# One block of a hybrid encoder on one core: three attention and gate steps, one load's page and some weight offsets in other places

## The chip, the cores and the metric

The kernel runs on one core of a Trainium2 chip. The metric is the device time of one execution in microseconds (us); of several runs the median counts. The kernel before has three runs: 2178.95, 2183.16 and 2185.89 us, median 2183.16.

## The reference, cut to what matters

One layer of a hybrid block on 512 frames of 2048 channels, all in float32:

```python
h = rms_norm(x, norm_mix_w)
q_a, k_a, v_a, q_g, k_g, v_g, r_g, gate_lr = split_cols(h @ w_in, IN_SPLITS)   # 6160 columns
y_a = chunked_band_attention(q_a, k_a, v_a, att_rel_bias)    # 16 heads of 64
o_g = gated_linear_attention(q_g, k_g, v_g, log_a)           # 4 heads, chunk by chunk
y_g = rms_norm(o_g, gla_norm_w) * silu(r_g)
x = x + concat([y_a, y_g]) @ w_out
u = causal_depthwise_conv(rms_norm(x, norm_ffn_w) @ w_ffn_up, w_ffn_conv, b_ffn_conv)
u_gate, u_val = split(u, 2)                                  # 5632 columns each
x = x + (gelu(u_gate) * u_val) @ w_ffn_down
g = sigmoid(rms_norm(x, norm_ple_w) @ w_ple_gate)
x = x + g * (p @ w_ple_proj)
out = rms_norm(x, final_norm_w)
```

In the attention a query sees its own chunk of 64 frames and the eight before it, with a learned bias by relative distance, and a softmax over them.

## The kernel before, in words

**Units, products, steps.** Nearly all time goes into matrix products. A unit makes two blocks of 128 output columns for all 512 frames. It does so with seven products of half-sized operands instead of eight (Strassen's scheme): P1, P2, P6, P5, P7, P3, P4, of which some take a sum of two weight blocks (S1 to S4) and some a sum or difference of two input blocks (N1, N2, T3, T4). A product is one step of a list of 704 steps (`steps`). In it TensorE runs 24 matmuls of 128 by 256 columns: eight blocks of the contraction, three times over, first the weights' high part with the input's high part, then the high part with the input's low part, then the weights' low part with the input's high part. So the low weights are first read by the 17th matmul.

The stages follow each other: `front` (the projection w_in; gate units and attention pairs), `pp` (per-layer embedding), `wo`, `up`, `dn0` to `dn2`, `pg`. The steps that matter here: 0 to 41 the linear-attention units, 42 to 90 the attention pairs' projections, 84 to 111 the gate units 0 to 3, 112 to 115 `pp`, 116 on `wo`, 172 on `up`, 648 on `pg`.

**Weights.** A block of weights (`l`, 512 KB) comes from memory into a page. Sums (`s`) are made by a load with an accumulating second DMA on GpSimd's queue, or on VectorE. Two steps ahead of a step, ACT copies the raw block into a high part (`w<-l`, `w<-s`) and VectorE subtracts it to give the low part (`w<-l,w`, `w<-s,w`). Both go to one of three slots, used in turn (step number modulo 3); a slot starts at 1024 columns times its number plus an offset, 24 unless `places` gives another for that step (line 546). `place` fills that table (line 983).

**Attention.** `attend(unit)` (line 810) gives a list of work items for one pair of heads: `high`, `low` and `low_copy` split the queries and keys, then three turns h, one for each of three groups of query tiles: `scores` (TensorE, `psc`), `soft` (VectorE and ACT), `normal` (VectorE divides by the sums), `turn` (TensorE transposes the result, `ptr`) and `evict` (ACT copies the transposes to `PT`), and at the end `values` (TensorE, `py`) and `result`. Turn 1 uses the buffer `scb`, turns 0 and 2 `sc`. Pair 0's items are counted from step 38, pair 7's from step 84.

**Gates.** A gate unit g (0 to 3) has its result multiplied by the linear attention's output, which lies in memory (`ond`). `load_on` (line 925) loads it into a page `on` of 512 KB; `after_gates` then has VectorE multiply (`u<-u,on`) and `store_pair` makes four sums (`tp`) and stores seven blocks of 128 KB (`mix_R..`, `mix_N..`, `mix_T..`) for the next stage. `page(ring, ...)` takes the next page of a ring of named pages: ring "c" has three pages at that place, ring "x" two.

**The order.** Each item has a step and a key: key 0 is before the split of the weights two steps ahead, 1 between its halves, 2 to 8 behind the step's matmuls, 9 after ACT or VectorE has added the product to its unit. TensorE, ACT and VectorE run in the order that this list gives, and each waits at its first unready instruction. Transfers are issued by SP, and accumulating ones by GpSimd; their order is made by a scheduler from its own estimates, so an edit can move a transfer past others. SP waits at the first one whose page, source or completion count isn't ready, and everything behind it waits too. Eight completion counters are used in turn, so an issue also waits for the landing of the eighth one before it.

Of the kernel before, what the change touches and what calls it, by code (L numbers as in the profile page):

```python
# [42 lines left out]
def encoder_block(ctx: ExitStack, tc: tile.TileContext, A, out):  # L43
# [5 lines left out]
    pg = ctx.enter_context(tc.tile_pool(name="pages", bufs=1))  # L49
# [53 lines left out]
    def page(ring, name, dt=F32, shape=(P, 1024)):  # L103
        tags = rings[ring]
        i = counts.get(ring, 0)
        counts[ring] = i + 1
        tag = tags[i % len(tags)]
        return page_pool(tag).tile(list(shape), dt, tag=tag, name=name)
# [3 lines left out]
    def page_pool(tag):  # L112
        return late[0] if tag in LATE else pg
# [221 lines left out]
    def xtile(op, g, name, dt=F32R):  # L335
        if (op, g) not in H_TAGS:
            return xa[0].tile([P, 2, 1024], dt, tag=f"{op}{g}", name=name)
        c = 2048 * H_TAGS.index((op, g))
        return h_all[:, c:c + 2048].rearrange("p (h n) -> p h n", h=2)
# [473 lines left out]
    def attend(unit):  # L813
        b, M = unit.u, {}
        o = unit.o

        def tile_(name, cols, dt=F32, tag=None, bufs=1):
            return att[0].tile([P, cols], dt, tag=tag or name, name=name, bufs=bufs)
# [8 lines left out]
        def high(s):  # L827
            for n in ("Q", "Kh", "Kl"):
                M[n, s] = tile_(f"{n}{s}", T + 64, F32R)[:, 16:16 + T] if n == "Q" else tile_(f"{n}{s}", T, F32R)
            a = slice(s * 64, s * 64 + 64)  # L830
            act.activation(M["Q", s][a], o[a, 0, :], AF.Copy, scale=0.125)
            for r in (a, slice(64 - s * 64, 128 - s * 64)):
                act.activation(M["Kh", s][r], o[a, 1, :], AF.Copy)
# [71 lines left out]
        def result():  # L905
            if b % 2 == 0:
                ypair[:] = [page("c", "yp").rearrange("p (s t) -> p s t", s=2)]
            act.activation(ypair[0][:, b % 2, :], M["y"], AF.Copy)

        done = 13 if b < 3 else 14 if b < 7 else 10  # L910
        items = [(2 + (b == 1), 7, load_e if b else lambda: None), (2, 2, lambda: high(0)), (2, 9, lambda: high(1)), (3, 1, low), (4, 2, low_copy), (9 - b // 7, 0, load_v),
                 (done, 4, values), (done + 1, 1, result)]
        if b % 2:
            items.append((done + 2, 1, lambda: store_pair(mixd, b // 2, ypair[0][:, 0, :], ypair[0][:, 1, :])))
        z = b == 0
        for h in range(3):
            t = (7 + z, 9 if b < 7 else 8, 11 if b < 7 else 9)[h]
            items += [(t, k, lambda f=f, h=h: f(h)) for t, k, f in (
                (5 + h + z * (h == 2), 6, scores), (6 + h + z * (h == 2), 1, soft), ((7, 8, 10 if b < 7 else 9)[h], 1, normal),
                (t, 5, turn), (t + 1, 1, evict))]  # L920
        return items

# [1 line left out]

    def load_on(unit):
        g = unit.u - 8
        unit.on = page("x" if g == 0 else "c", "on").rearrange("p (s t) -> p s t", s=2)
        nc.sync.dma_start(unit.on, ond[g])

    def after_gates(unit):  # L930
        g = unit.u - 8

        def times():
            vec.tensor_tensor(unit.o, unit.o, unit.on, ALU.mult)

        def pair():
            ops = store_pair(mixd if g < 2 else None, 4 + g, unit.o[:, 0, :], unit.o[:, 1, :])
            if g >= 2:
                tails[g - 2] = ops

        load = [] if g == 2 else [(0, 0, lambda: load_on(unit))]
        return load + [(0, 1, lambda: act.activation(unit.o, unit.o, AF.Silu)), (2 * (g in (1, 2)), 2, times), (2 * (g in (1, 2)), 3, pair)]
# [25 lines left out]
    wo = stages[2]  # L968
    units = [u for st in stages for u in st.units]
    steps = []  # L970
    base = {}
# [9 lines left out]
    places = {}  # L981

    def place(i):
        places[i + (1 - i) % 3] = 0

    for unit, at in ((front.units[13], 1), (front.units[14], -2)):
        place(base[unit] + at)
    plain = [i for i, (_, p) in enumerate(steps) if p == "PP"]
    for i in plain:
        if i % 3 < 2:  # L990
            places[i] = (72, 8)[i % 3]
    for st in stages[2:]:
        for at in (0 if st.name == "wo" else 3, *range(13 if st.name == "up" else 16, 7 * len(st.units) - 14, 21)):
            place(base[st.units[0]] + at)

    agenda = [[] for _ in range(len(steps) + 60)]
    now = [0]
    for a, b in zip(stages[2:], stages[3:]):
        i0 = base[a.units[-1]]
        for n, p in enumerate(PLAIN):  # L1000
            op = PRODUCTS[p][1]
            for g in range(2):
# [3 lines left out]
                at = 2 * n + (11 if g else 8)  # L1006
                k = 3
                if g and b.chained and op in ("R21", "T4"):
                    at, k = max(at, 15), 0 if op == "R21" else 3
                if b.chained and op == "N1":  # L1010
                    at = 17 + g
# [110 lines left out]
    for n in range(2):  # L1122
        u = stages[-1].units[n - 2]
        at = end + 4 + n
# [517 lines left out]
    agenda[base[front.units[4]] + 9].append((0, first_bias))  # L1642
    agenda[base[front.units[4]] + 12].append((0, open_attention))
    agenda[base[front.units[14]] + 5].append((0, lambda: load_on(front.units[14])))
    use_rings(FRONT_RINGS)
    for i, (unit, prod) in enumerate(steps[:-4]):
        st = unit.stage
# [21 lines left out]
        if i - len(steps) in EARLY:  # L1669
            p, op, g = EARLY[i - len(steps)]  # L1670
            t = xtile(op, g, "last")
# [247 lines left out]
```

## Time and profile before

| | before |
|---|---|
| median of three runs | 2183.16 us |
| the profiled execution | 2181.47 us, its span 2179.7 us |
| mean granted clock of TensorE | 0.998 |
| TensorE busy | 2167.8 us, 99% |
| VectorE busy | 1860.8 us, 85% |
| ACT busy | 1333.4 us, 61% |
| DMA | 566.64 MB, 55.4% of 16 engines by SP's and ACT's queue, 31.0% by GpSimd's |

The span is the time from the first to the last instruction of one execution; a share is of that span. The granted clock is 1.00 at 2.4 GHz, and a mean between 0.5 and 1.00 is a stretch with some of it at 1.2 GHz. In timelines, the number in front is the start in us, then comes the duration, the engine, the line, the operation and "out<-in" by the names in the program; in brackets behind it, how long the engine idled before and what ended that. "x24" is 24 instructions in a row. A step's matmuls overlap, so the ends that the rows give run over into the next step's start; the distance of two starts is the cadence.

### The profile page before, as it was taken

The page shows a single profiled execution, that of the slowest core. Times are in us where ns is not written, and L with a number is a line of the kernel's source. Part 1 is how long each engine was busy: PE and PEld are TensorE (multiplying, and loading weights), DVE is VectorE, ACT ScalarE, POOL GpSimd, SP SyncE. Part 2 cuts the span into 40 slices and gives each one's busy share as a digit, 9 for nine tenths or more (in the row PEclk, how much of TensorE's full clock was granted, in tenths as well). Part 3 has the DMA queues.
Part 4 walks back from the last instruction along what each step waited for, and adds up shares of the span by engine and source line. Part 5 has one row for each costly group of instructions (what it writes and reads, how often), then busy time and mean ns, then how long its engine had stood idle before and what let it go on. Part 6 is the DMA issues. An engine that isn't in the chain of part 4 may idle for free.

```text
span 2179.7 us, 45707 instructions
## 1 busy us (share of the span) xinstructions
PE 2167.8 (99%) x18262; PEld 2123.8 (97%) x18262; DVE 1860.8 (85%) x2549; ACT 1333.4 (61%) x1976; POOL 216.2 (10%) x263
## 2 busy tenths in 40 slices
PE   9999999999999999999999999999999999999998
PEld 7889999999999999999999999999999999999998
DVE  6977778888698889999888888888898687898998
ACT  6664567876665765555555555555564554666766
POOL 1111011111100001110111111011100101000010
PEclk9999999999999999999999999999999999999999
DMA  7988788889978978999999989989986976979996
GB/s 245 271 220 232 217 242 227 231 245 251 365 272 266 363 223 240 269 265 262 261 239 261 257 257 252 257 244 250 270 302 187 309 222 178 332 247 341 304 291 230
DMA packets 199973, 566.64 MB, mean 260 GB/s; under 512 B 22384, under 2 KB 61552, under 8 KB 199760
## 3 DMA queue, kind: packets, MB, share of 16 engines
q1 hardware_dynamic: 163232, 436.00, 55.4%
q0 software_dynamic: 34944, 125.32, 31.0%
q8 instruction: 143, 2.34, 0.4%
q10 hardware_dynamic: 1584, 2.40, 0.3%
q14 instruction: 70, 0.57, 0.1%
HBM read 490.23 MB, written 127.93 MB: 284 GB/s over the span
## 4 chain that ended last, share of the span: by engine, by line
PE 96%; DVE 2%; ACT 1%; DMA 1%; issue 1%; POOL 0%; ACTq 0%; DVEq 0%; POOLq 0%
PE accA L64 48%; PE accC L64 24%; PE accB L64 12%; PE v L64 4%; PE vaA L64 2%; PE pp L64 1%; PE vaC L64 1%; PE py L64 1%; PE psc L64 1%; PE ptr L64 1%; PE po L64 1%; PE vaD L64 0%; PE vaB L64 0%; DMA s<-in_w_blk 0%; DVE w L64 0%
## 5 line engine op out<-in xcount | busy, mean ns | idle before, releaser
L64 PE MATMUL accA<-h,w 128*128 128x256 f32 x5088 | 612.2, 277 | 0.2
L64 PEld LDWEIGHTS accA<-h,w 128*128 128x128 f32 x5088 | 594.6, 188 | 1.7 <-ACT u L64 0.3
L64 DVE TENSOR_TENSOR w<-s,w 128x1024 fp32r<-128x1024 f32 (+1 forms) x381 | 457.5, 1202 | 81.6 <-ACT w L64 81.1
L64 PE MATMUL accC<-h,w 128*128 128x256 f32 x4248 | 509.0, 276 | 0.0
L64 PEld LDWEIGHTS accC<-h,w 128*128 128x128 f32 x4248 | 494.2, 188 | 0.3
L64 DVE TENSOR_TENSOR w<-l,w 128x1024 fp32r<-128x1024 f32 (+1 forms) x320 | 383.1, 1197 | 63.3 <-ACT w L64 61.8
L64 ACT ACTIVATE w<-l 128x1024 fp32r<-128x1024 f32 (+1 forms) x320 | 332.3, 1039 | 165.6 <-PE accC L64 112.3
L64 ACT ACTIVATE w<-s 128x1024 fp32r<-128x1024 f32 (+1 forms) x381 | 395.0, 1037 | 23.5 <-PE accB L64 11.6
L64 ACT ACTIVATE u<-accA 128x256 f32<-128x256 f32 x302 | 114.5, 379 | 365.1 <-PE accA L64 362.5
L64 DVE TENSOR_TENSOR s<-s,l 128x1024 f32<-128x1024 f32 (+1 forms) x176 | 211.3, 1201 | 9.9 <-DMA s<-in_w_blk 7.7
L64 POOL DMA_DIRECT2D s<-in_w_up x84 | 73.3, 872 | 742.0 <-DMA s<-in_w_up 224.2
L64 DVE SCALAR_TENSOR_TENSOR cv<-u,cw,cv 128x511 f32<-128x511 f32 (+1 forms) x176 | 131.6, 748 | 3.1
L64 PE MATMUL accB<-up_R,w 128*128 128x256 f32 x1056 | 127.7, 277 | 0.0
L64 PE MATMUL accA<-up_R,w 128*128 128x256 f32 x1056 | 126.7, 276 | 0.0
L64 PE MATMUL accA<-up_N,w 128*128 128x256 f32 x1056 | 126.5, 276 | 0.0
L64 PEld LDWEIGHTS accB<-up_R,w 128*128 128x128 f32 x1056 | 124.0, 188 | 0.0
L64 PEld LDWEIGHTS accA<-up_R,w 128*128 128x128 f32 x1056 | 122.9, 188 | 0.0
L64 PEld LDWEIGHTS accA<-up_N,w 128*128 128x128 f32 x1056 | 122.8, 188 | 0.0
L64 ACT ACTIVATE u<-accC 128x256 f32<-128x256 f32 x98 | 37.5, 383 | 94.4 <-PE accC L64 94.1
L64 PE MATMUL v<-w,h 128*128 128x512 f32 x384 | 88.1, 390 | 0.1
L64 PEld LDWEIGHTS v<-w,h 128*128 128x128 f32 x384 | 71.8, 188 | 15.6 <-ACT g_t L64 0.5
L64 ACT ACTIVATE cv<-u,cw 128x512 f32<-128x512 f32 x88 | 67.1, 810 | 28.1 <-DVE u L64 26.6
(315 smaller groups left out, 2834.2 us busy)
## 6 DMA issues: line engine op xcount, KB each, us to landing
l<-in_w_up SPq DMA_DIRECT2D x132, 512.0 KB, 7.3
s<-in_w_up SPq DMA_DIRECT2D x84, 512.0 KB, 4.8
s<-in_w_up POOLq DMA_DIRECT2D x84, 512.0 KB, 7.0
l<-in_w_dn SPq DMA_DIRECT2D x56, 448.0 KB, 5.5
l<-in_w_blk SPq DMA_DIRECT2D x48, 512.0 KB, 6.0
s<-in_w_blk SPq DMA_DIRECT2D x32, 512.0 KB, 4.8
s<-in_w_blk POOLq DMA_DIRECT2D x32, 512.0 KB, 7.9
l<-in_w_out SPq DMA_DIRECT2D x28, 512.0 KB, 4.9
```

The costliest lines, as they stand in the source:

```text
L64: ins = f(*args, **kw)
```

## The change

Four things are edited.

- Pair 0 (b = 0): the second turn comes one step later, at step 48 instead of 47, and `high(1)` has another key. Pair 7 (b = 7): the second turn comes at step 93 instead of 92, the third at 94 instead of 93, the values at 95 instead of 94; the normalising stays.
- Gate unit 1's load takes a page of ring "x" instead of "c". The units 2 and 3 thereby get other pages of "c".
- A place is given by the step itself, with offset 64 in the third slot and 0 in the first, where it was always the second slot with 0.
- The places: 117 (offset 64) instead of 118 in `wo`, 186 (64) instead of 187 and every 21 steps from 211 instead of 208 in `up`, and a new 661 in `pg`. The others stay.

```diff
--- before.py
+++ after.py
@@ -907,16 +907,16 @@
                 ypair[:] = [page("c", "yp").rearrange("p (s t) -> p s t", s=2)]
             act.activation(ypair[0][:, b % 2, :], M["y"], AF.Copy)
 
-        done = 13 if b < 3 else 14 if b < 7 else 10
-        items = [(2 + (b == 1), 7, load_e if b else lambda: None), (2, 2, lambda: high(0)), (2, 9, lambda: high(1)), (3, 1, low), (4, 2, low_copy), (9 - b // 7, 0, load_v),
+        done = 13 if b < 3 else 14 if b < 7 else 11
+        items = [(2 + (b == 1), 7, load_e if b else lambda: None), (2, 2, lambda: high(0)), (2, 9 if b else 2, lambda: high(1)), (3, 1, low), (4, 2, low_copy), (9 - b // 7, 0, load_v),
                  (done, 4, values), (done + 1, 1, result)]
         if b % 2:
             items.append((done + 2, 1, lambda: store_pair(mixd, b // 2, ypair[0][:, 0, :], ypair[0][:, 1, :])))
         z = b == 0
         for h in range(3):
-            t = (7 + z, 9 if b < 7 else 8, 11 if b < 7 else 9)[h]
+            t = (7 + z, 9 + z, 10 + (b < 7))[h]
             items += [(t, k, lambda f=f, h=h: f(h)) for t, k, f in (
-                (5 + h + z * (h == 2), 6, scores), (6 + h + z * (h == 2), 1, soft), ((7, 8, 10 if b < 7 else 9)[h], 1, normal),
+                (5 + h + z * (h == 2), 6, scores), (6 + h + z * (h == 2), 1, soft), ((7, 8, 9 + (b < 7))[h], 1, normal),
                 (t, 5, turn), (t + 1, 1, evict))]
         return items
 
@@ -924,7 +924,7 @@
 
     def load_on(unit):
         g = unit.u - 8
-        unit.on = page("x" if g == 0 else "c", "on").rearrange("p (s t) -> p s t", s=2)
+        unit.on = page("x" if g < 2 else "c", "on").rearrange("p (s t) -> p s t", s=2)
         nc.sync.dma_start(unit.on, ond[g])
 
     def after_gates(unit):
@@ -981,17 +981,23 @@
     places = {}
 
     def place(i):
-        places[i + (1 - i) % 3] = 0
+        places[i] = (64, 0)[i % 3]
 
     for unit, at in ((front.units[13], 1), (front.units[14], -2)):
-        place(base[unit] + at)
+        place(base[unit] + at + (1 - base[unit] - at) % 3)
     plain = [i for i, (_, p) in enumerate(steps) if p == "PP"]
     for i in plain:
         if i % 3 < 2:
             places[i] = (72, 8)[i % 3]
     for st in stages[2:]:
-        for at in (0 if st.name == "wo" else 3, *range(13 if st.name == "up" else 16, 7 * len(st.units) - 14, 21)):
-            place(base[st.units[0]] + at)
+        b0 = base[st.units[0]]
+        for at in (1 if st.name == "wo" else 3, *range(16, 7 * len(st.units) - 14, 21)):
+            place(b0 + at + ((1 - b0 - at) % 3 if at > 1 else 0))
+        if st.name in ("up", "pg"):
+            after = max(i for i in places if i <= b0 + 18)
+            place(after - (4 if st.name == "up" else 3))
+            if st.name == "up":
+                del places[after]
 
     agenda = [[] for _ in range(len(steps) + 60)]
     now = [0]
```

TensorE's order around the first pair's second and third turn (`scb` the second, `sc` the third, `acc` the steps' matmuls; steps 47 to 49), before:

```order
L64 MATMUL accC<-in_R_1043,w 128x256 x2
L64 MATMUL ptr<-ident,scb 128x128 x6
L64 MATMUL accA<-h_100,w 128x256 x24
L64 MATMUL accA<-in_R_643,w 128x256 x4
L64 MATMUL accA<-in_R_760,w 128x256 x4
...
L64 MATMUL accA<-in_R_760,w 128x256 x4
L64 MATMUL ptr<-ident,sc 128x128 x6
L64 MATMUL psc<-Kh_3352,Q_3351 128x512
```

and now:

```order
L64 MATMUL accC<-in_R_1043,w 128x256 x2
L64 MATMUL accA<-h_100,w 128x256 x24
L64 MATMUL ptr<-ident,scb 128x128 x6
L64 MATMUL accA<-in_R_643,w 128x256 x4
L64 MATMUL accA<-in_R_760,w 128x256 x4
...
L64 MATMUL accA<-in_R_760,w 128x256 x4
L64 MATMUL ptr<-ident,sc 128x128 x6
L64 MATMUL psc<-Kh_3352,Q_3351 128x512
```

The six transposes of the second turn have moved behind the whole step 48; the third turn stays where it was, now with only step 49 between.

TensorE's order at the last pair (`py` the values), steps 92 to 95, before:

```order
L64 MATMUL accB<-in_R_1043,w 128x256 x2
L64 MATMUL ptr<-ident,scb 128x128 x6
L64 MATMUL accA<-h_100,w 128x256 x24
L64 MATMUL ptr<-ident,sc 128x128 x6
L64 MATMUL accC<-h_100,w 128x256 x24
L64 MATMUL py<-PT,va 64x128 x20
L64 MATMUL accA<-h_100,w 128x256 x24
L64 MATMUL accC<-in_R_671,w 128x256 x2
```

and now:

```order
L64 MATMUL accB<-in_R_1043,w 128x256 x2
L64 MATMUL accA<-h_100,w 128x256 x24
L64 MATMUL ptr<-ident,scb 128x128 x6
L64 MATMUL accC<-h_100,w 128x256 x24
L64 MATMUL ptr<-ident,sc 128x128 x6
L64 MATMUL accA<-h_100,w 128x256 x24
L64 MATMUL py<-PT,va 64x128 x20
L64 MATMUL accC<-in_R_671,w 128x256 x2
```

Both turns and the values stand one step later.

VectorE's order at the last pair's sums (`tp_6047` before, `tp_6090` now) and gate 0's multiply (`on_6097`, now `on_6085`), before:

```order
L64 TENSOR_TENSOR w_99<-l22_5642,w_99 128x1024
L64 TENSOR_TENSOR u_5842<-u_5842,accA_5776 128x256
L64 TENSOR_TENSOR tp_6047<-yp_5847 128x256 x2
L64 SCALAR_TENSOR_TENSOR tp_6047<-tp_6047,yp_5847 128x256 x2
L64 TENSOR_TENSOR w_99<-l11_5716,w_99 128x1024
L64 TENSOR_TENSOR u_5842<-u_5842,accC_5968 128x256
L64 TENSOR_TENSOR s2_6099<-s1_5912,l11_5716 128x1024
L64 TENSOR_TENSOR w_99<-l12_5875,w_99 128x1024
L64 TENSOR_TENSOR u_5464<-u_5464,on_6097 128x1024
```

and now:

```order
L64 TENSOR_TENSOR w_99<-l22_5642,w_99 128x1024
L64 TENSOR_TENSOR u_5842<-u_5842,accA_5776 128x256
L64 TENSOR_TENSOR w_99<-l11_5716,w_99 128x1024
L64 TENSOR_TENSOR u_5842<-u_5842,accC_5958 128x256
L64 TENSOR_TENSOR s2_6087<-s1_5904,l11_5716 128x1024
L64 TENSOR_TENSOR tp_6090<-yp_5847 128x256 x2
L64 SCALAR_TENSOR_TENSOR tp_6090<-tp_6090,yp_5847 128x256 x2
L64 TENSOR_TENSOR w_99<-l12_5875,w_99 128x1024
L64 TENSOR_TENSOR u_5464<-u_5464,on_6085 128x1024
```

The four `tp` instructions stand behind the S2 sum now.

SP's order at the gates' loads (`on_6142` is gate 1's, `on_6309` and `on_6602` those of 2 and 3; `l12_6090`, now `l12_6078`, is a later unit's block; `u_5464`, `tp_6129` are gate 0's results), before:

```order
L64 DMA l11_6088<-in_w_blk 128x1024
L310 DMA mix_N10_118<-tp_6047 128x256
L310 DMA mix_T30_120<-tp_6047 128x256
L310 DMA mix_N20_122<-tp_6047 128x256
L310 DMA mix_T40_124<-tp_6047 128x256
L928 DMA on_6142<-ond_202 128x1024
L64 DMA s3_6176<-in_w_blk 128x1024
L64 DMA l12_6090<-in_w_blk 128x1024
L310 DMA mix_R111_113<-u_5464 128x256
L310 DMA mix_R211_115<-u_5464 128x256
L310 DMA mix_R221_117<-u_5464 128x256
```

and now:

```order
L64 DMA l11_6076<-in_w_blk 128x1024
L928 DMA on_6085<-ond_202 128x1024
...
L928 DMA on_6309<-ond_202 128x1024
L928 DMA on_6602<-ond_202 128x1024
L310 DMA mix_N10_118<-tp_6090 128x256
...
L310 DMA mix_T40_124<-tp_6090 128x256
L64 DMA s3_6176<-in_w_blk 128x1024
L310 DMA mix_R111_113<-u_5464 128x256
...
L310 DMA mix_T41_125<-tp_6129 128x256
L928 DMA on_6142<-ond_202 128x1024
L64 DMA l22_6206<-in_w_blk 128x1024
L64 DMA l11_6210<-in_w_ple_proj 128x1024
```

Gate 1's load stood ahead of S3 and gate 0's stores and now stands behind them; the loads of the gates 2 and 3, which came after row `l11_6282` some twenty places later, are ahead of it; L11 of the next unit (`l11_6076`) is ahead of gate 0's load.

## Rows read from the trace of the kernel before

**Rows 1.** The page: engines' busy time; then the chain's shares by engine.

```profile
PE 2167.8 (99%) x18262; PEld 2123.8 (97%) x18262; DVE 1860.8 (85%) x2549; ACT 1333.4 (61%) x1976; POOL 216.2 (10%) x263
...
PE 96%; DVE 2%; ACT 1%; DMA 1%; issue 1%; POOL 0%; ACTq 0%; DVEq 0%; POOLq 0%
```

**Rows 2.** Three windows, one step each: us, PE busy, PEclk, DMA share, GB/s.

```profile
788.13:790.96 2.83, 2.83 (x27) 1.00 0.44 35
790.96:793.76 2.80, 2.80 (x27) 1.00 0.99 252
793.76:796.48 2.72, 2.72 (x27) 1.00 1.01 361
```

**Rows 3.** TensorE's timeline, first pair: start, us, instruction, idle before and releaser.

```profile
341.89 1.03 PE L64 MATMUL ptr<-ident,scb 128*128 128x128 f32 x6 [2.13 <-ACT PT L64]
342.68 4.60 PE L64 MATMUL accA<-h,w 128*128 128x256 f32 x24
...
349.95 0.81 PE L64 MATMUL ptr<-ident,sc 128*128 128x128 f32 x6
```

**Rows 4.** Windows around it, all engines: us, busy, PEclk, DMA share.

```profile
341.00:348.00 7.00, 6.11 (x38) 5.94 (x39) 6.76 (x15) 6.68 (x18) 0.00 (x0) 0.76 1.08 253
348.00:350.00 2.00, 2.00 (x19) 2.00 (x19) 1.83 (x2) 0.79 (x1) 0.00 (x0) 1.00 1.06 240
```

**Rows 5.** TensorE's timeline, last pair and the step at 549.

```profile
521.16 0.55 PE L64 MATMUL ptr<-ident,sc 128*128 128x128 f32 x3
521.94 0.63 PE L64 MATMUL ptr<-ident,sc 128*128 128x128 f32 x3 [0.22 <-DVE mx L64]
...
549.61 2.88 PE L64 MATMUL accC<-in_R,w 128*128 128x256 f32 x24
```

**Rows 6.** VectorE's timeline around the two gate units.

```profile
535.23 1.23 DVE L64 TENSOR_TENSOR s<-s,l 128x1024 f32<-128x1024 f32 x1 [1.19 <-DMA s<-in_w_blk]
...
537.51 1.22 DVE L64 TENSOR_TENSOR u<-u,on 128x1024 f32<-128x1024 f32 x1
...
545.69 1.23 DVE L64 TENSOR_TENSOR u<-u,on 128x1024 f32<-128x1024 f32 x1 [0.49 <-DMA on<-ond]
...
548.43 1.22 DVE L64 TENSOR_TENSOR w<-s,w 128x1024 fp32r<-128x1024 f32 x1
```

**Rows 7.** ACT's timeline, first pair: evictions of the turns.

```profile
341.25 1.07 ACT L64 ACTIVATE PT<-ptr 128x512 f32<-128x512 f32 x2
...
344.91 0.85 ACT L64 ACTIVATE PT<-ptr 128x384 f32<-128x384 f32 x2
```

**Rows 8.** VectorE's timeline, first pair: the last normalising.

```profile
347.22 0.29 DVE L64 TENSOR_SCALAR sc<-sc,mx 128x128 f32<-128x128 f32 x1
```

**Rows 9.** SP's queue, 529 to 540: when each transfer is issued.

```profile
529.30 0.43 SPq L64 DMA_DIRECT2D l<-in_w_blk  x1
...
536.02 0.32 SPq L928 DMA_DIRECT2D on<-ond  x1
539.08 0.33 SPq L64 DMA_DIRECT2D s<-in_w_blk  x1
```

**Rows 10.** DMA, 536 to 542: queues (packets, MB, engine share); issues (us to landing).

```profile
q0 software_dynamic: 265, 0.96, 80.3%
q1 hardware_dynamic: 374, 0.47, 25.0%
...
on<-ond SPq DMA_DIRECT2D x1, 512.0 KB, 9.6
s<-in_w_blk SPq DMA_DIRECT2D x1, 512.0 KB, 7.8
```

**Rows 11.** DMA, 548 to 550: queues.

```profile
q1 hardware_dynamic: 800, 0.73, 104.4%
q0 software_dynamic: 3, 0.01, 7.6%
```

**Rows 12.** DMA, 560.6 to 561.1: an issue.

```profile
on<-ond SPq DMA_DIRECT2D x1, 512.0 KB, 4.6
```

## Prediction

> **What bounds the kernel now.** I read the page's busy times and its chain of waits first. TensorE is busy 2167.8 of 2179.7 us and 96% of the chain that ended last lies on it [rows 1], so a change counts only where it opens or closes a gap on TensorE, or makes its matmuls slower. Then I went through TensorE's timeline for starts that come later than the cadence. A step of 24 matmuls takes 2.72 us [rows 2], 0.113 us for a matmul. Three places bear on this diff.
>
> First pair: the second turn's transposes start at 341.89 after 2.13 us in which TensorE waits for ACT's evictions of the turn before, and the step behind them takes 4.60 us [rows 3]. The windows say why: a granted clock of 0.76 over 341 to 348, 1.00 after it [rows 4], so part of that stretch ran at the lower of the two levels, 1.2 GHz, after the wait. Last pair: the third turn comes in two halves, the second 0.22 us behind VectorE's normalising [rows 5]. Slow steps without any wait: 2.83 us for a step in the up stage, 2.80 for the step where the page offset changes, 2.72 after it [rows 2].
>
> Nothing waits on TensorE near 545, but the cover there is thin. VectorE multiplies the second gate unit by its load (`on`, 512 KB) at 545.69, after 0.49 us of waiting for that load, and the product's low weights come two instructions later, at 548.43 [rows 6].
>
> **The change part by part.**
>
> *First pair, second turn one step later.* Step 48's 24 matmuls now fill the gap: they start where the cadence puts them, at 339.76 (341.89 less 2.13), and end near 342.5. The two banks are free by then (ACT's evictions run from 341.25 for 1.07 us [rows 7]), so the second turn costs its 0.6 us and step 49 ends near 345.8. Now the third turn is late: VectorE's last normalising ends at 347.51 [rows 8], and VectorE has no gap before it, so an earlier TensorE does not pull it forward. The third turn starts at 347.5 instead of 349.95 [rows 3]: 2.4 us gained, about 0.2 of it lost because the next pair's scores wait for an eviction of 0.85 us [rows 7] that now lies behind step 49. That is 2.2 us if the clock stays up. But the new wait is 345.8 to 347.5, 1.7 us, close to the 2.13 after which a step took 4.60 instead of 2.88 on the same view, 1.7 us more [rows 3]. If that repeats, 0.5 us is left. All wait and all clock together would return 2.4 + 1.7 = 4.1 us at most. No row has a wait of 1.7 us with its clock, so I take the middle of 0.5 and 2.2: **-1.3 us**.
>
> The new key of the second head's copies moves nothing on ACT, VectorE or TensorE.
>
> *Last pair, third turn and values one step later.* The turns' excess of 0.22 us of wait and the 0.6 us that the split turn costs over a whole one go: -0.85 us at 530. This reaches the end only if nothing waits afterwards, and the next part makes something wait. There is also a small price: VectorE's four `tp` instructions (1.5 us, the gap between 545.69 + 1.23 and 548.43 [rows 6]) now stand behind the S2 sum, which itself waits 1.19 us for a transfer [rows 6].
>
> *Page of the second gate load.* This is what decides. Before, the load is issued at 536.02, ahead of S3 at 539.08 [rows 9], and takes 9.6 us [rows 10]. In the new order on SP it stands behind the loads of gates 2 and 3, behind L11 of the next unit, S3 and seven stores of gate 0's pair, and it waits for the landing of S3 (the eighth transfer before it). Step by step:
> - S3 landed at 539.08 + 7.8 = 546.9 [rows 9, 10]. Two loads more (gates 2 and 3) and one less (gate 1) are ahead of it, 0.5 MB. SP's queue alone moves 0.73 MB in 2 us [rows 11], so 0.5 MB is 1.4 us: S3 lands at about 548.3, and the gate load is issued then.
> - It has seven stores of 128 KB in front of it in the queue and 512 KB of its own: 1.4 MB, 3.9 us. The undisturbed load of gate 2 takes 4.6 us [rows 12]. It lands at 552.2 to 552.9; I take 552.5.
> - Before, it landed about 545.7, when VectorE's multiply started [rows 6]: 6.8 us later. Behind that multiply VectorE's queue holds the four `tp`, then the low weights of step 103, done at 549.65 before (548.43 + 1.22 [rows 6]), 556.5 now. The stores of gate 1 wait too, but nobody needs them yet.
> - TensorE starts step 103 at 549.61 [rows 5] and reads low weights after two of its three passes, 16 matmuls: 549.61 + 16 x 0.113 = 551.42. Cover 1.8 us, so the wait is 6.8 - 1.8 = 5.0 us **against before's position**; the last pair's 0.85 us has vanished in it, and a delay of gate 0's load (L11, issued at 529.30 before [rows 9], now stands ahead of it) vanishes in it too.
> - A wait of that length is over the 2.13 us of [rows 3], so one slow step follows: +1.7 us. The gain at the first pair stays beside it, because these transfers are issued when pages come free, which moves with TensorE.
>
> Together **+6.7 us**. The bounds: if SP's stores drain early, S3 takes as little as the 4.6 us of [rows 12], to 543.7, and the gate load as little again: landing 548.3, 2.6 us late, a wait of 0.8 us and no slow clock. The other end is a load that takes 9.6 us again [rows 10]: 548.3 + 9.6 = 557.9, a wait of 10.4 us, with the slow step 12.1.
>
> One rule of the Trainium skill speaks for that upper end. While an accumulate of GpSimd's queue ran, from 536 to 542, that queue (q0) sent 265 packets for 0.96 MB and 80.3% of the engines' time, SP's (q1) 374 packets in 25.0% [rows 10], and the load in that stretch took 9.6 us against 4.6 at 560 [rows 12]. "DMA: Bandwidth & Descriptors", section "Queues, rings and completion order", says that each engine takes turns between the queues that have work, a packet at a time. The trace agrees roughly, 1.4 packets of SP's to one. S3's own accumulate starts when S3 has landed, as the gate load does, so by the rule the load would share again and the sum would be the slower rival's below. Against it: before, S3's accumulate was issued at about 547.4 too, and in 548 to 550 SP's queue still had 104.4% of the time and the other 3 packets [rows 11].
>
> *Places of the offset.* The page that is taken at another offset moves one step ahead: at 117 (was 118), 186 (was 187), and one more at 661, before the slow steps there have run. A slow step costs 2.83 - 2.72 = 0.11 us [rows 2]; about three are saved: **-0.35 us**. The new offset is 64 in the third slot, where before it was 0 in the second. No row shows 64 in that slot. If it does not end the slow spell, some 39 steps up to the next place stay 0.11 us slow: +4.3 us instead. I take the gain, since the place of before ends its spell at once (2.80, then 2.72), and the new one differs from its neighbours' offset as that one did.
>
> **Sum.** -1.3 - 0.35 + 6.7 = +5.1 us. Against the profiled execution (2181.47 us, its span 2179.7) that is 2186.6; against the median of the runs, 2183.16, 1.7 us higher, it is 2188.2. I say 2187.
>
> **Rivals.**
> - *The gate load lands in time* (or is covered by a TensorE that is itself late). For it: its page is free early, and a transfer of 4.6 us occurs [rows 12]. Against: the order behind S3 and seven stores. It decides if the landing is before 547.5. Then -1.3 - 0.85 - 0.35 = -2.5 us: 2179.0 to 2180.7.
> - *The gate load shares the engines with S3's accumulate*: the slower side. Place: VectorE's multiply of gate 1; price 12.1 us; it decides once the landing is later than about 556. -1.3 - 0.35 + 12.1 = +10.4: 2191.9 to 2193.6. For it the 9.6 us of [rows 10], against it [rows 11].
> - *Offset 64 leaves the spell running*: +5.1 + 0.35 + 4.3 = +9.8: 2191.3 to 2193. For it only that no row shows this offset in this slot.
>
> **How the numbers follow.** Forecast 0.55, load in time 0.29, load shared 0.11, offset 0.05. 0.3% (6.5 us, about what a measurement of this kernel can tell from no change) puts the bounds at 2176.6 and 2189.7. The first rival stays inside even with the whole 4.1 us at the first pair (2176.2 to 2177.9, just at the edge): faster 0.03. The forecast with its wait between 0.8 and 10.4 has somewhat over a fifth beyond 2189.7, 0.12, and the two slower rivals add 0.16: slower 0.28. Same 0.69. The range is 2178 to 2193; the forecast's own is 2181 to 2192.
>
> **What would show it.** First pair: the second turn at about 342.5 without a wait, a wait of 1.5 to 2 us before the third turn on VectorE's normalising, and a granted clock in 341 to 348 that tells 0.5 from 2.2. Last pair: one block of six transposes, without a wait, and the accumulator steps near 530 earlier. Gates: the load of gate 1 issued after S3 has landed, VectorE's second multiply waiting some microseconds for it, and a wait of about 5 us on TensorE in the middle of step 103 with a slow step behind; if the multiply starts before 547, the forecast is wrong and the time is below before's. Places: no step over 2.80 us behind 117, 186 and 661.

## The result, and the profile after

The changed kernel takes 2188.88 us (median of 8 runs, 2187.41 to 2190.2) against 2181.80 us for the kernel before (8 runs, 2178.95 to 2185.89). The ratio is 1.0032 with a 95% interval of 1.0021 to 1.0043: 7.1 us slower. The profiled execution took 2187.41 us, its span 2185.5, that is 5.9 us over the profiled one of before. The prediction said 2187 us, 5.1 us over the profiled execution of before.

TensorE's busy time rose by 2.2 us against [rows 1] and its share of the chain fell from 96 to 95%; the rest of the loss is waiting. The page's rows:

```profile
PE 2170.0 (99%) x18262; PEld 2125.2 (97%) x18262; DVE 1860.7 (85%) x2549; ACT 1333.7 (61%) x1976; POOL 216.3 (10%) x263
...
PE 95%; ACT 2%; DVE 1%; DMA 1%; issue 1%; ACTq 0%; POOL 0%; DVEq 0%; SPq 0%; POOLq 0%
```

To see where the time went, I took each step's start on TensorE from both traces, counted from step 0, and subtracted (us; a negative number is a lead over the kernel before). This is worked out from the timelines:

```
step              44     50     57     96    100    105    112    120    190    490    497    703
after           0.10  -2.37  -0.55  -1.15  -1.05   4.93   4.93   4.82   4.71   4.68   5.26   5.27
```

So 2.5 us were won at the first pair and 1.8 of them given back within seven steps; 0.6 was won at the last pair; 6.1 were lost at the gates, steps 96 to 105; 0.2 was won by the places and 0.6 lost in the first down-projection. Another 0.5 us lies ahead of step 0, which the change doesn't touch.

**First pair.** TensorE's timeline, start and duration, with the wait and its releaser in brackets:

```profile
340.21 2.99 PE L64 MATMUL accA<-h,w 128*128 128x256 f32 x24
343.04 0.82 PE L64 MATMUL ptr<-ident,scb 128*128 128x128 f32 x6
343.62 3.07 PE L64 MATMUL accA<-in_R,w 128*128 128x256 f32 x24
346.92 0.63 PE L64 MATMUL ptr<-ident,sc 128*128 128x128 f32 x3 [0.23 <-DVE mx L64]
347.77 0.63 PE L64 MATMUL ptr<-ident,sc 128*128 128x128 f32 x3 [0.22 <-DVE mx L64]
348.59 0.50 PE L64 MATMUL psc<-Kh,Q 128*128 128x512 f32 x1 [0.18 <-ACT PT L64]
...
366.55 3.09 PE L64 MATMUL accC<-in_R,w 128*128 128x256 f32 x24 [0.23 <-ACT u L64]
371.15 3.07 PE L64 MATMUL accA<-h,w 128*128 128x256 f32 x24 [1.50 <-ACT PT L64]
```

Against [rows 3], step 48 fills the wait, the second turn starts without one, and the third turn waits 0.23 and 0.22 us, in two halves, for VectorE's two halves of the normalising. The step behind the second turn takes 3.07 us and not 4.60. The window says that the clock stayed up, where [rows 4] had 0.76:

```profile
341.00:348.00 7.00, 6.54 (x54) 6.03 (x52) 6.73 (x16) 6.93 (x16) 0.00 (x0) 1.00 1.06 215
```

Then TensorE waits 1.50 us at step 55 for ACT's `PT`. Two views lead back to the cause. VectorE's timeline shows the softmax of the second pair's second head 2.15 us late; the releaser named, TensorE's scores, had long been done, and a wait for several things is put down to one of them:

```profile
350.21 0.69 DVE L64 CUSTOM_DVE_ANT_0 sc<-psc,bias 128x512 f32<-128x512 f32 x1
...
353.24 0.69 DVE L64 CUSTOM_DVE_ANT_0 sc<-psc,bias 128x512 f32<-128x512 f32 x1 [2.15 <-PE psc L64]
```

The other operand is the bias. Its four loads were issued between 339.63 and 342.50, and the last one needed 10.6 us, to 353.1 (issues of 342.4 to 342.7: KB each, us to landing):

```profile
bias<-in_bias SPq DMA_DIRECT2D x1, 128.0 KB, 10.6
```

In the kernel before, the last one took about as long (issues of 340.9 to 341.1), but it landed at 351.39, and VectorE came to that softmax only at 352.15, so nobody waited for it:

```profile
bias<-in_bias SPq DMA_DIRECT2D x1, 128.0 KB, 10.4
```

**Last pair.** One block of six transposes each and no wait, as against [rows 5]:

```profile
520.41 0.82 PE L64 MATMUL ptr<-ident,scb 128*128 128x128 f32 x6
...
523.90 0.82 PE L64 MATMUL ptr<-ident,sc 128*128 128x128 f32 x6
```

**Gates.** SP's queue shows gate 1's load behind S3 and the seven stores, issued at 546.59 instead of 536.02 [rows 9]:

```profile
541.06 0.33 SPq L64 DMA_DIRECT2D s<-in_w_blk  x1
541.49 2.69 SPq L310 DMA_DIRECT2D mix_R<-u  x3
...
546.59 0.32 SPq L928 DMA_DIRECT2D on<-ond  x1
```

S3 took 5.5 us, the gate load 4.0 (issues of 541.0 to 541.4 and of 546.5 to 547.0):

```profile
s<-in_w_blk SPq DMA_DIRECT2D x1, 512.0 KB, 5.5
```

```profile
on<-ond SPq DMA_DIRECT2D x1, 512.0 KB, 4.0
```

So S3 landed at 546.57, 0.02 us before the gate load was issued. VectorE waits 1.95 us for gate 0's load and 3.66 us for gate 1's, where [rows 6] had none and 0.49, and step 103's low weights come at 553.38 instead of 548.43:

```profile
539.29 1.23 DVE L64 TENSOR_TENSOR u<-u,on 128x1024 f32<-128x1024 f32 x1 [1.95 <-DMA on<-ond]
...
545.77 1.22 DVE L64 TENSOR_TENSOR w<-s,w 128x1024 fp32r<-128x1024 f32 x1
550.65 1.23 DVE L64 TENSOR_TENSOR u<-u,on 128x1024 f32<-128x1024 f32 x1 [3.66 <-DMA on<-ond]
...
553.38 1.22 DVE L64 TENSOR_TENSOR w<-s,w 128x1024 fp32r<-128x1024 f32 x1
```

TensorE waits 0.45 us in the middle of step 100, 2.60 us in the middle of step 103, 0.36 us before step 104, and that step takes 4.40 us:

```profile
543.30 1.21 PE L64 MATMUL accA<-h,w 128*128 128x256 f32 x8 [0.45 <-DVE w L64]
...
550.00 2.05 PE L64 MATMUL accC<-in_R,w 128*128 128x256 f32 x16
554.65 1.20 PE L64 MATMUL accC<-in_R,w 128*128 128x256 f32 x8 [2.60 <-DVE w L64]
556.21 4.40 PE L64 MATMUL accA<-h,w 128*128 128x256 f32 x24 [0.36 <-DVE u L64]
```

Part of that step ran at the lower of the two clock levels, 1.2 GHz: over 556 to 561 the granted clock was 0.67 (us, busy times, PEclk):

```profile
556.00:561.00 5.00, 4.79 (x29) 4.82 (x30) 3.80 (x5) 0.35 (x2) 0.00 (x0) 0.67 1.13 344
```

**Places.** At 186, the place with offset 64 in the third slot, the step before it takes 2.83 us, it itself 2.80 and the next 2.72, as one step later in the kernel before [rows 2]:

```profile
790.60:793.42 2.82, 2.82 (x26) 1.00 0.24 85
793.42:796.22 2.80, 2.80 (x26) 1.00 0.37 26
796.22:798.94 2.72, 2.72 (x26) 1.00 1.00 273
```

### The profile page after: what moved, and what is told of

It reads as the page before. It is cut to its first block, busy times and chain, and to the rows that moved or that the text cites. A ratio compares the mean times of both kernels' runs of the same rounds, so it can differ in the third digit from the quotient of the medians.

```text
span 2185.5 us, 45699 instructions
## 1 busy us (share of the span) xinstructions
PE 2170.0 (99%) x18262; PEld 2125.2 (97%) x18262; DVE 1860.7 (85%) x2549; ACT 1333.7 (61%) x1976; POOL 216.3 (10%) x263
## 4 chain that ended last, share of the span: by engine, by line
PE 95%; ACT 2%; DVE 1%; DMA 1%; issue 1%; ACTq 0%; POOL 0%; DVEq 0%; SPq 0%; POOLq 0%
PE accA L64 47%; PE accC L64 23%; PE accB L64 12%; PE v L64 4%; PE vaA L64 1%; PE pp L64 1%; PE vaC L64 1%; PE psc L64 1%; PE py L64 1%; PE ptr L64 1%; PE po L64 1%; PE vaD L64 0%; PE vaB L64 0%; DMA mix_R<-yp 0%; DMA h<-h_T 0%
## 5 line engine op out<-in xcount | busy, mean ns | idle before, releaser
L64 DVE TENSOR_TENSOR u<-u,accC 128x256 f32<-128x256 f32 x102 | 42.8, 420 | 50.7 <-PE accC L64 50.5
```

The lines of the kernel that those rows point to most:

```text
L64: ins = f(*args, **kw)
```

## The experiments

Each ratio is to runs of the kernel before on the same chip, with its 95% interval. Step leads are counted as above.

**1. The change without the page (e1_page_back).**

```diff
-        unit.on = page("x" if g < 2 else "c", "on")
+        unit.on = page("x" if g == 0 else "c", "on")
```

> The changed kernel with gate unit 1's load back in ring c. Theory (the page's ring puts this load behind S3 and seven stores, and that wait with the slow step is the whole loss): the waits at steps 100 and 103 and the slow step go, some 5 to 6 us, so the time is 0.5 to 1.5 us below the kernel before's: -0.6 at the last pair and about 0 net at the first pair. Rival (the moved third turn and tp sums of the last pair make the gates late, the page adds little): at least 2 us of wait stay near step 103 and the time is 1 us or more above the kernel before's.

Measured: 2183.20 us, 1.0003 (0.9995 to 1.0012), against 1.0032 for the whole change. The load goes out ahead of S3, and VectorE's multiply no longer waits:

```profile
546.11 1.22 DVE L64 TENSOR_TENSOR u<-u,on 128x1024 f32<-128x1024 f32 x1
```

The page is the loss. The expected gain of 0.5 to 1.5 us did not come, though: the lead of 1.41 us at step 96 shrinks to 0.03 at step 112. Step 100's low weights come 0.08 us late, and from there to the next place of the offset every step takes 2.83 us (the first and the last of twelve):

```profile
540.72:543.55 2.83, 2.83 (x27) 1.00 1.03 270
571.82:574.64 2.82, 2.82 (x26) 1.00 1.04 414
```

**2. The page alone (e2_page_only).** The kernel before with the line of experiment 1 the other way round.

> The kernel before with gate unit 1's load in ring x and nothing else. Theory: the load is issued after S3 has landed, VectorE's multiply waits for it, and the time rises by 5 to 7 us over the kernel before. Rival (it takes the last pair's later sums to make it late): a rise of under 2 us.

Measured: 2192.13 us, 1.0051 (1.0036 to 1.0066), by the medians 9.4 us more (0.43%; the six runs spread from 2191.36 to 2200.42, and the ratio is not that of the medians), above what either theory said. The rival falls: the page needs no help from the last pair. Here the load was issued at 550.44 and took 7.9 us, beside S3's accumulate (issued 549.30), where it took 4.0 in the changed kernel; VectorE waits 11.19 us and TensorE 8.78 (this profiled execution is 4.2 us above the kernel's median, so its waits are probably longer than those of a median run):

```profile
558.37 1.23 DVE L64 TENSOR_TENSOR u<-u,on 128x1024 f32<-128x1024 f32 x1 [11.19 <-DMA on<-ond]
```

```profile
562.38 2.07 PE L64 MATMUL accC<-in_R,w 128*128 128x256 f32 x8 [8.78 <-DVE w L64]
```

**3. The first pair alone (e3_first_pair_only).**

```diff
-            t = (7 + z, 9 if b < 7 else 8, 11 if b < 7 else 9)[h]
+            t = (7 + z, 9 + z if b < 7 else 8, 11 if b < 7 else 9)[h]
```

> The kernel before with the first pair's second turn one step later and nothing else. Theory (the 2.4 us won at step 50 are given back at steps 53 to 55, because the second pair's bias, the fourth of four loads, lands no earlier and VectorE, ACT and the turn behind it wait for it): 2.4 us won at step 50, at most 0.6 us left at step 57, the time within 0.6 us of the kernel before. Rival (the late bias of the one profiled execution was chance, or came from the rest of the change): about 2 us are left at step 57 and in the time.

Measured: 2181.33 us, 0.9995 (0.9987 to 1.0004). In the profile 2.49 us are won from step 44 to 50 and 0.74 given back by step 57. The theory fails: 1.75 us are left at step 57, not 0.6 at most, and the time is 1.4 us below the kernel before, though the interval still touches 1. The rival's "about 2 us" is nearer. What is given back follows the landing of the last bias load: 0.74 us with 351.21 here, 1.63 with 352.87 in experiment 1, 1.82 with 353.12 in the changed kernel. So the late bias belongs in part to the rest of the change or to the execution.

**4. The places alone (e4_places_only).** The kernel before with the changed block of `place`.

> The kernel before with the new places of the offset and nothing else. Theory (from the two traces: -0.07 in wo, -0.08 in up, about 0 in pg, and +0.55 in dn0, where six steps of 0.11 us appear ahead of step 496): +0.3 us. Rival (the prediction: three slow steps saved): -0.35 us. Both are near what the runs can tell; the trace's steps decide.

Measured: 2183.20 us, 0.9999 (0.9990 to 1.0007). In the trace the step leads change by -0.10 in `wo` (steps 116 to 120), -0.11 in `up` and -0.02 in `pg`: the prediction's sign, two thirds of its size. No slow steps appear in `dn0`; those of the changed kernel (491 to 496, +0.58) appear in experiment 2 too, which has the old places, so they don't come from the new ones.

This kernel has the first pair of before, and its trace corrects a reading of [rows 3, 4]: the wait is 2.12 us again, but the step behind it takes 2.98 us, at a granted clock of 1.00. In experiment 2, with a wait of 2.00 us, the clock was 0.76 and the step took 4.61 us. First the timeline of experiment 4, then the window 341 to 348 (us, busy times, PEclk) of 4 and of 2:

```profile
341.70 1.03 PE L64 MATMUL ptr<-ident,scb 128*128 128x128 f32 x6 [2.12 <-ACT PT L64]
342.50 2.98 PE L64 MATMUL accA<-h,w 128*128 128x256 f32 x24
```

```profile
341.00:348.00 7.00, 6.29 (x54) 6.12 (x55) 6.76 (x15) 6.93 (x18) 0.00 (x0) 1.00 1.06 231
```

```profile
341.00:348.00 7.00, 5.43 (x32) 5.25 (x33) 6.73 (x15) 6.70 (x16) 0.00 (x0) 0.76 1.07 245
```

That changes what the first pair's edit is worth. Experiment 4 has the old first pair, and yet from step 44 to 57 it is 1.98 us ahead of the kernel before, 1.72 of it at the step behind the wait, where the clock stayed up; experiment 8, also with the old pair and at 1.00, is 1.99 us ahead. The changed kernel is 0.65 us ahead over the same steps. Measured against an old first pair at full clock, its edit has thus lost 1.3 us by step 57.

**5. Two accumulates out of the bias load's way (e5_sums_later).** Experiment 1's kernel, with the background sums from the eighth on seven steps later:

```diff
-        agenda[11 + 5 * i].append((0, f))
+        agenda[11 + 5 * i + (7 if i > 6 else 0)].append((0, f))
```

> The kernel of e1_page_back (the change without the page) with the background sums for the output projection, from the eighth on, seven steps later, so that two 512 KB accumulates are no longer in the queues while the second pair's bias is loaded (340 to 353). Theory (bias lands late because of these accumulates, and that gives back the first pair's gain): the fourth bias load lands before 350 instead of 353, VectorE's wait of about 2 us at 353 goes, at least 1 us more of the 2.5 us is left at step 57, and the time is 1 to 2 us below e1_page_back. Rival (ACT's and VectorE's own work between 350 and 370 is the limit, the bias only fills a gap): no more than 0.4 us is kept at step 57.

Measured: 2185.27 us, 1.0013 (1.0004 to 1.0022). The half of the theory that it was made for holds: the last bias load takes 6.3 us instead of 10.6 and lands at 348.0, VectorE's wait is gone, and all of the 2.49 us is still there at step 57 (lead 2.59):

```profile
bias<-in_bias SPq DMA_DIRECT2D x1, 128.0 KB, 6.3
```

```profile
350.33 0.69 DVE L64 CUSTOM_DVE_ANT_0 sc<-psc,bias 128x512 f32<-128x512 f32 x1
...
351.21 0.69 DVE L64 CUSTOM_DVE_ANT_0 sc<-psc,bias 128x512 f32<-128x512 f32 x1
```

The time is wrong. What the trace shows for it is that two later sums now fall on the gates (experiments 9 and 10 move them away). VectorE's S2 sum waits 5.27 us for S1's accumulate, and TensorE waits 2.29 us at step 99 and 1.80 us at step 100:

```profile
536.64 1.23 DVE L64 TENSOR_TENSOR s<-s,l 128x1024 f32<-128x1024 f32 x1 [5.27 <-DMA s<-in_w_blk]
```

```profile
540.52 1.19 PE L64 MATMUL accB<-in_R,w 128*128 128x256 f32 x8 [2.29 <-DVE w L64]
...
545.32 1.77 PE L64 MATMUL accA<-h,w 128*128 128x256 f32 x8 [1.80 <-DVE w L64]
```

**6. The last pair alone (e6_last_pair_only).**

```diff
-        done = 13 if b < 3 else 14 if b < 7 else 10
+        done = 13 if b < 3 else 14 if b < 7 else 11
-            t = (7 + z, 9 if b < 7 else 8, 11 if b < 7 else 9)[h]
+            t = (7 + z, 9, 11 if b < 7 else 10)[h]
```

> The kernel before with the last pair's third turn and values one step later and nothing else. Theory (0.6 to 1.5 us are won at step 96, but the later sums and the gate load behind L11 make step 100's low weights late by a trifle, and from a matmul that waited the steps stay 0.11 us slower up to the next place of the offset, step 112): the trace shows steps 100 to 111 at 2.83 us and the time is within 1 us of the kernel before. Rival (the win stays): 0.6 to 1.5 us below it, with steps at 2.72.

Measured: 2183.51 us, 1.0008 (1.0000 to 1.0017). 0.60 us is won from step 91 to 96 and 0.44 of it is still there at step 112, at 2.72 us a step: the expected slow steps did not come here. 2.1 us are lost at steps 162 to 175, far from the edit: VectorE waits 3.06 and 0.88 us for two accumulates (sums for `wo`), TensorE then 0.31 us in the middle of step 162, and from step 165 the steps take 2.83 us up to the next place. Step 162 is longer than its 2.72 us in experiments 2, 5, 7, 10 and 11 too (3.09 to 4.68), with this edit or without it. Why those accumulates come late there, I did not find.

**7. Experiment 5 with one more place, at step 102 (e7_sums_later_and_place).**

```diff
+    place(base[front.units[14]] + 4)
```

> The kernel of e5_sums_later with one more place of the offset, at step 102 (offset 64). Theory (a place ends the slow spell that begins at step 100): two slow steps in place of about twelve, 1.0 us less than e5_sums_later, and 2 to 3.5 us below the kernel before. Rival (the spell has another cause, such as the transfers of that stretch): steps 103 to 111 stay at 2.83 us and the time is that of e5_sums_later.

Measured: 2183.53 us, 1.0007 (0.9998 to 1.0016): 1.7 us less than experiment 5, but not below the kernel before, where the theory wanted 2 to 3.5. One slow step, 101, and 2.72 us from 103 on, as the theory wants; but experiment 5's own profile had no slow steps there (a step of 3.96 us followed its wait of 1.80 us), so the comparison doesn't show what the place is worth. In this profile TensorE waited 4.29 us at step 99.

**8. The later sums alone (e8_sums_later_only).** The kernel before with experiment 5's line.

> The kernel before with only the background sums of e5_sums_later seven steps later. Theory (without the first pair's change TensorE is late by itself, so an earlier bias finds nobody waiting): within 0.5 us of the kernel before. Rival (the accumulates cost time wherever they stand): 1 us or more faster.

Measured: 2183.54 us, 1.0008 (0.9999 to 1.0016): no gain, so the rival falls; the 1.4 us are more than the theory's 0.5. In its profile 3.6 us go at steps 99 to 112, so the later sums cost at the gates here too.

**9. The first pair and the places, with four sums elsewhere (e9_first_pair_and_four_sums).** The kernel before with the edits of 3 and 4, the new key of `high(1)` and:

```diff
-        agenda[11 + 5 * i].append((0, f))
+        agenda[{7: 54, 8: 55, 16: 118, 17: 121}.get(i, 11 + 5 * i)].append((0, f))
```

> The kernel before with the first pair's second turn one step later, the new places of the offset, and four of the background sums' steps elsewhere: two (steps 46 and 51) at 54 and 55, out of the bias load's way, and two (91 and 96) at 118 and 121, out of the gates' way; gate 1's page and the last pair as before. Theory (the first pair's gain was lost to the late bias, and e5_sums_later lost at the gates because its later sums fell there): 2.4 to 2.9 us are kept at step 57 and no wait over 0.3 us comes at steps 99 to 104, so the time is 2 to 3.5 us below the kernel before. Rival (the gates' stretch is limited by its own loads, whatever else runs): TensorE waits 2 us or more there and the time is within 1 us of the kernel before.

Measured: 2181.79 us, 0.9992 (0.9983 to 1.0001). The lead is 2.95 us at step 57 and 3.53 from step 96 to 112, without a wait: theory on both places, and no floor from the gates' own loads. VectorE's S2 sum waits only 1.13 us for S1, 4.99 us earlier than in experiment 5:

```profile
531.65 1.23 DVE L64 TENSOR_TENSOR s<-s,l 128x1024 f32<-128x1024 f32 x1 [1.13 <-DMA s<-in_w_blk]
...
541.53 1.22 DVE L64 TENSOR_TENSOR u<-u,on 128x1024 f32<-128x1024 f32 x1
```

1.4 us of that lead go at steps 488 to 490, in waits for weights. The time is 1.3 us below the kernel before, not 2 to 3.5, and the lead has to be read with care: it is counted from the one execution with the clock of 0.76. From step 44 to 57 this kernel is 2.60 us ahead of it, and only 0.6 ahead of experiment 4, where the clock stayed up. The 0.58 us from step 91 to 96 came without the last pair's edit. This version beats the changed kernel (1.0032) clearly; against the kernel before the interval still touches 1.

**10. The same with the last pair (e10_same_with_last_pair).** Experiment 9 with experiment 6's edit.

> The kernel of e9_first_pair_and_four_sums with the last pair's third turn and values one step later too. Theory: 0.6 us more at step 96, and the sums behind S2 do no harm once the two accumulates are gone from there: 0.3 to 1.5 us below e9. Rival (the later sums and gate 0's load behind L11 make step 99 or 100 wait for its low weights): no faster than e9.

Measured: 2181.00 us, 0.9992 (0.9983 to 1.0001), the same as 9. The rival's waits are there, 0.58 us at step 99 and 0.77 at step 100, with 2.83 us a step from 104 to 111: the lead of 3.51 us at step 96 is 0.50 at step 112. The theory's 0.6 us more at step 96 did not come (3.51 us against 3.53 in experiment 9), so in this profile the last pair's change only costs, as the rival said; in the times the two kernels can't be told apart.

**11. The whole change with the four sums elsewhere (e11_change_and_four_sums).**

> The changed kernel with the four background sums elsewhere as in e9: gate 1's load still in ring x. Theory (the load waits for the four stores of the last pair's sums and for S3, and these for the transfers ahead of them; without two accumulates in the stretch they land sooner): the wait for the load at step 103 falls from 2.6 us with its slow step to under 1.5 us, but it stays the last thing to land, and the time is 0 to 4 us above e10. Rival (the order on SP alone sets it): the wait is as long as in the changed kernel, and the time 5 to 8 us above e10.

Measured: 2185.89 us, 1.0015 (1.0006 to 1.0024), 4.9 us above experiment 10. VectorE's wait for gate 1's load falls from 3.66 to 2.41 us, TensorE's from 2.60 to 1.66, and the step behind it takes 2.98 instead of 4.40 us:

```profile
550.07 1.23 DVE L64 TENSOR_TENSOR u<-u,on 128x1024 f32<-128x1024 f32 x1 [2.41 <-DMA on<-ond]
```

```profile
554.07 1.21 PE L64 MATMUL accC<-in_R,w 128*128 128x256 f32 x8 [1.66 <-DVE w L64]
555.63 1.62 PE L64 MATMUL accA<-h,w 128*128 128x256 f32 x12 [0.35 <-DVE u L64]
```

Transfers beside it lengthen the wait, the order makes it: both readings have a part, and neither range of the time was right to the end.

## Why the prediction was right

**The step that decided.** The load of gate 1 was issued 0.02 us after S3 had landed, behind the seven stores, as worked out. S3 landed at 546.6 (predicted 548.3) and the gate load at 550.6 (552.5): the 1.4 us for the extra 0.5 MB ahead of S3 did not show, since S3 was issued 2.0 us later than before but took 5.5 us and not 7.8. Low weights were done at 553.38 + 1.22 = 554.6 (predicted 556.5). Against the kernel before, the loss by step 105 is 4.93 us; the prediction's was 6.7 - 1.3 = 5.4. The slow step is there, 4.40 us (1.5 over the usual 2.88 on this view, predicted 1.7). That the two sums agree so well is in part luck. In the prediction's own terms, against the position of before, the wait was 3.4 us (the loss at step 104; 2.60 us idle in the middle of step 103, where a wait of about 5 was to be seen) and not 5.0, and with the slow step the gates come to 4.9 and not 6.7. The 1.3 us taken off for the first pair is not seen beside that: the 4.93 already holds whatever the first pair left. The two errors of 1.8 and 1.3 us go opposite ways. Experiments 1 and 2 show that the page is the cause: taken out, the loss goes; alone, it costs 9.4 us.

What the prediction got wrong is the page: the rival "load in time" called it free early. By the order in which the code asks for pages, ring x hands out two in turn to gate 0's load, to `tp` of the last pair, to `tp` of gate 0 and then to gate 1's load, so this load gets the page of the last pair's `tp` and can't start before its four stores have landed, the last at 545.4 in the changed kernel. S3's landing at 546.6 came later still, so the trace shows the order on SP as the last wait; the page alone would have made the load over 9 us later than the 536.02 of [rows 9].

**First pair.** The gain of 2.2 us to step 50 was 2.5. The failing term is the 1.7 us of wait before the third turn, which was 0.45 (step 49 ended at 346.7, not 345.8, and the two halves of the turn start as VectorE finishes each half), and so the fear for the clock. The bound of 2.4 + 1.7 = 4.1 us counts the clock twice: the 2.4 us run from a third turn at 349.95 that the slow step had already made late (348.04 in experiment 4). And taking the gain as kept to the end failed: the prediction followed TensorE only to the next pair's scores. 1.8 us are given back at steps 53 to 55, since VectorE waits for the bias of those scores (353.1 us, 351.4 before). Experiment 5 shows that: with two accumulates moved, bias 5 us earlier, all is kept; so it is in experiments 9 to 11. Against the -1.3 that was taken, -0.65 is left in the changed kernel, and +1.3 against an old first pair at full clock.

**The clock.** The 1.7 us that the prediction put down as part of the first pair's cost were one execution's: with the same wait, 2.00 to 2.13 us, the granted clock of 341 to 348 was 0.76 in three traces (before, experiments 2 and 6) and 1.00 in two (experiments 4 and 8). What decides it stays open.

**Last pair.** 0.6 us won, predicted 0.85: the 0.22 us of wait were counted twice, since they lie inside the 0.6 us that the split turn takes longer [rows 5]. It vanished at the gates as said; experiment 10's profile shows the edit costing there. Nor is 0.6 a fixed sum: in the old order steps 92 to 95 took 15.45 us in the kernel before, 14.87 in experiments 8 and 9, and 15.90 to 16.29 in 2, 3 and 4; in the new order 14.85 in every trace.

**Places.** -0.35 predicted, -0.23 in the trace of experiment 4. Offset 64 ends the slow steps as 0 did, so that rival is out. Of three places two paid; at 661 almost nothing was won, as steps 662 and 663 still took 3.53 and 2.91 us (3.64 and 2.82 before). The 0.58 us in `dn0` is not theirs.

**Shared engines.** This rival did not happen in the changed kernel (4.0 us). In experiment 2 it did: 7.9 us beside S3's accumulate. S3's accumulate was in the queues in both. In the changed kernel the load was issued 0.53 us ahead of it (4.0 us), in experiment 11 0.06 us behind it (4.7), in experiment 2 1.14 us behind it (7.9). That is a pattern of three traces which no run tested by itself. If it holds, the short load hung on half a microsecond, and a chance of about one in ten for the rival was low.

**The sum.** Predicted +5.1 us; the profiled executions differ by 5.9 and the medians by 7.1 us. Of the 5.9, 0.5 lies ahead of step 0 and 0.6 in `dn0`, and neither was in the sum. The first is scatter as far as the traces tell: step 0 starts between 175.42 us (the kernel before) and 176.34 in the thirteen profiles. The medians differ by 1.1 us more than the profiled executions because the changed kernel's profiled execution was the fastest of its eight, 1.5 us below their median, and that of before only 0.3 below. So the sum fell 2 us short of the medians. Most of the chances, 0.69, lay on a difference within 0.3%; the ratio, 1.0032, is just past that line.

## What to carry to other kernels

When a transfer gets another page, look for who held that page last and when that one's stores land; a ring of two can put a load behind work that has nothing to do with it. A gap closed on the bounding engine is only worth what the next operand from memory allows: follow the engines that feed it five to ten steps on, and look for loads that are limited by the other queue. Before moving background transfers, see which stretch has no room for them; with experiment 5's later sums the kernel was 2 us slower than experiment 1, through the gates, and experiment 9's cost nothing there. And before crediting an edit with a gap it closes, look at the same gap in a second execution of the kernel before: here 1.7 of 2.5 us were the clock of one execution (experiment 4).

## What the hardware showed that was not expected

- After a wait of 2.0 to 2.1 us in the same place, TensorE's granted clock around it was 0.76 in three executions and 1.00 in two, with the step behind it at 4.3 to 4.6 us or at 2.98.
- A wait of 0.08 us in the middle of step 100 was followed by steps at 2.83 instead of 2.72 us, without any further wait, up to the next step with another offset, 112 (experiment 1). The 0.45 us in the same step of the changed kernel were followed by three such steps too, the 0.36 us ahead of its step 104 were not. What starts them stays open; a run of them that reached a step with another offset ended there.
